# Down projection: the second block group takes six tiles in place of four, the plain group ahead of it two in place of four

## The chip, the cores and the metric

The kernel runs on one core of a Trainium2 chip. The metric is the device time of one execution in microseconds (us), the median of the runs; lower is better.

## The reference

Two layers of an encoder on 1040 frames (1024 and 16 learned ones in front) of width 1024. In each layer a mixing part (gated linear attention and softmax attention with a forget gate) is added to the residual `h`, and then a gated feed-forward part with a causal convolution. The change concerns the last product of that part, the down projection by `w_down`, from 2816 gated channels back to 1024:

```python
def conv_ffn(x, w_up, conv_w, conv_b, w_down):
    h = x @ w_up
    ...
    u, g = jnp.split(hc, 2, axis=-1)
    return (jax.nn.silu(g) * u) @ w_down
...
h = h + conv_ffn(rms_norm(h, ffn_norm[i]), w_up[i], conv_w[i], conv_b[i], w_down[i])
```

## The kernel before, in words

Everything is float32. A factor is split into a high part in TensorE's reduced format and a low part (the rest), and each product is three matmuls (`mm3`): high by high (L261), low weight by high (L262), high weight by low (L263). ScalarE makes the high part with a cast, VectorE the low part with a subtraction. Activations lie with channels on the 128 partitions and frames along the free axis.

**Tiles of the down projection.** The gated activation has 22 tiles of 128 channels; each was written to DRAM (`actd`) when it was made. The output has 8 tiles (m = 0 to 7), `hm0` to `hm7`, which hold the residual in DRAM. The two halves of the frames have 520 columns each in layer 0, which take two matmuls of 260, and 512 in layer 1, which take one. The 22 tiles are gone through in groups, listed in `GROUPS` as (kind, first tile, number of tiles); the last three tiles (`LAST`, 19 to 21) belong to `down_last`, which is not changed.

- A plain group (`"n"` or `"r"`, function `plain`) makes for each output tile and each half one product: all its gated tiles, three matmuls and one or two pieces each, into one of four two-bank PSUM tiles, p((2m+h) mod 4). The kind `"n"` copies the result out and adds it to `hm` in DRAM by an accumulating DMA of GpSimd (L1717). The kind `"r"` adds it on VectorE (L1713) into the residual tile `h0` to `h7`, which `load_residual` (L1688) has asked for on SP's queue.
- A block group (`"s"`, function `down_blocks`) takes its tiles as two halves (nk = half their number), two output tiles (2j and 2j+1) and two halves of the frames as a 2 by 2 block product, and makes seven products (p = 1 to 7) where eight would stand, from sums and differences of weights and of activations. Products of four pairs j run one after the other in a sequence that overlaps neighbouring pairs. The operands of the activations are `x1` to `x7`: `prepare` loads the gated tiles (`st`), combines them (L1546) and splits them (ScalarE L377, VectorE L378), in rounds of up to two tiles of each half. The weights come by `block_raws` (L1129) and `block_operand` (combinations at L1144, split at L1162 and L1163), asked for four products ahead (`AHEAD`); only for nk = 2 the raw weights of the next pair are asked for earlier (`ensure`). The results are `du` (tile 2j) and `dg` (tile 2j+1). `hand_on` adds them to `hm` by an accumulating DMA of GpSimd (L1617, before the residual is loaded) or to the residual tile on VectorE (L1614, after).

The order is: plain group of tiles 0 to 2, block group 3 to 10, plain group, block group, last three tiles.

**What sets the order.** TensorE's instructions stand in the order in which the program writes them. The other engines' instructions are ordered by a scheduler from the same text, so they shift with the code. All large tiles (`st`, `ah`, `al`, `x1` to `x7`, `du`, `dg`, `h0` to `h7`) share one list of 33 slots: `Slots.get` takes the slot that came free first, and a new user of a slot waits until its last user is done with it. For a `du` or `dg` of the first block group, that is when its accumulating DMA has landed.

```python
id = next((i for i in self.free if i in first), None) or next(i for i in self.free if i not in self.lent)
...
hT.append(s.get(F32, f"h{k}", first=ids))
nc.sync.dma_start(hT[k][:, o0:T], self.hm[k][:, o0:T])
...
nc.gpsimd.dma_start(self.hm[m][:, o0:T], x[:, o0:T], accum_op=ALU.add)
going.append((i + LANDING, x))
```

`pump` lets `prepare` run on whenever enough slots are free, so operands of the second block group are made during the first block group and the plain group behind it.

Of the kernel before, what the change touches and what calls it, by code (L numbers as in the profile page):

```python
# [48 lines left out]

GROUPS, LAST = (("n", 0, 3), ("s", 3, 8), ("r", 11, 4), ("s", 15, 4)), (19, 3)
HALVES, HALVES_LAST, HALVES_OUT = (0, 520, 520), (8, 524, 516), (16, 528, 512)
AHEAD = 4
LANDING = 4
# [1894 lines left out]
```

## Time and profile before

| | before |
|---|---|
| median of 3 runs | 2471.43 us (2471.32 to 2474.28) |
| the profiled execution | 2473.53 us, its span in the trace 2471.5 us |
| mean granted TensorE clock | 0.998 |
| plain group of four tiles, layer 0 | 1119.6 to 1165.5 us |
| second block group, layer 0 | 1165.5 to 1205.8 us |
| plain group of four tiles, layer 1 | 2340.5 to 2384.7 us |
| second block group, layer 1 | 2384.7 to 2423.6 us |

Times in rows are us from the span's start, unless marked ns. PE is TensorE, PEld its weight loads, DVE is VectorE, ACT is ScalarE, POOL is GpSimd, SP is SyncE, whose queue carries the loads. In a row of a timeline stand start, duration, engine, line, operation, output<-inputs without their numbers, shape and count, and in brackets the idle time of the engine before it and what released it. In a row of windows stand the window, the sum and each engine's busy time (with its count of instructions), the granted clock (1.00 is full speed), the DMA engines' busy share and GB/s. "st<-actd SPq ... , 260.0 KB, 3.7" is a group of transfers with the size of one and the median time from issue to landing.

### The profile page before, as it was taken

To read this page: it belongs to the slowest core of one execution; us is meant where nothing else is said; L and a number is where in the kernel's file an instruction comes from. 1 tells how busy PE (TensorE), PEld (TensorE's weight loads), DVE (VectorE), ACT (ScalarE), POOL (GpSimd) and SP (SyncE) were. 2 spreads that over 40 slices of the span, in tenths; PEclk is the share of its full clock that TensorE was granted. 3 is DMA by queue.
4 is the path that set the end of the run, shared out by engine and by line. 5 is a ranking of instruction groups with operands and counts; after the bars stand their busy time and mean duration, and the time that the engine had idled before them with its cause. 6 is when DMAs were issued, how large, how long until landed. Compare 5 with 4: busy or idle time off the path is not lost.

```text
span 2471.5 us, 47309 instructions
## 1 busy us (share of the span) xinstructions
PE 2440.1 (99%) x18286; PEld 2358.4 (95%) x18286; DVE 1873.4 (76%) x3769; ACT 1318.1 (53%) x2857; POOL 384.9 (16%) x565
## 2 busy tenths in 40 slices
PE   9999999999999999999999999999999999999998
PEld 8999999999999999999999999999999999998887
DVE  8665776869988888855866666777699888887667
ACT  7345766646555555642543456666465555556433
POOL 2023433210000000100220234331100000001002
PEclk9999999999999999999999999999999999999999
DMA  3222134443322224764312222243433212247722
GB/s 131 74 84 76 43 95 130 126 124 104 119 76 83 83 73 144 185 161 140 118 47 74 80 78 71 71 142 108 146 84 116 91 65 90 82 151 184 210 71 88
DMA packets 121680, 260.39 MB, mean 105 GB/s; under 512 B 15248, under 2 KB 37008, under 8 KB 121456
## 3 DMA queue, kind: packets, MB, share of 16 engines
q1 hardware_dynamic: 97008, 182.18, 23.8%
q0 software_dynamic: 22288, 72.81, 10.5%
q8 instruction: 143, 2.34, 0.4%
q10 hardware_dynamic: 2160, 2.38, 0.3%
q14 instruction: 81, 0.66, 0.1%
HBM read 176.74 MB, written 67.80 MB: 99 GB/s over the span
## 4 chain that ended last, share of the span: by engine, by line
PE 48%; issue 31%; DVE 13%; ACT 4%; DMA 2%; POOL 1%; SPq 0%; DVEq 0%; POOLq 0%; ACTq 0%
PE mm L261 7%; PE mm L263 7%; PE mm L262 7%; PE down L262 4%; PE down L261 4%; PE down L263 4%; PE av L780 3%; PE tr L754 2%; PE S L718 1%; DVE x L1188 1%; DVE S L721 1%; PE S L719 1%; ACT P L733 1%; DVE lo L1163 1%; DMA raw<-in_wm_dram 1%
## 5 line engine op out<-in xcount | busy, mean ns | idle before, releaser
L262 PE MATMUL up<-x,lo 128*128 128x260 f32 x2240 | 632.0, 282 | 0.9 <-DVE lo L1163 0.8
L261 PE MATMUL up<-x,hi 128*128 128x260 f32 x2240 | 632.0, 282 | 0.1
L263 PE MATMUL up<-x,hi 128*128 128x260 f32 x2240 | 632.0, 282 | 0.0
L262 PEld LDWEIGHTS up<-x,lo 128*128 128x128 f32 x2240 | 421.9, 188 | 1.4 <-DVE lo L1163 1.3
L261 PEld LDWEIGHTS up<-x,hi 128*128 128x128 f32 x2240 | 421.9, 188 | 0.4 <-ACT hi L1162 0.3
L263 PEld LDWEIGHTS up<-x,hi 128*128 128x128 f32 x2240 | 422.1, 188 | 0.0
L1162 ACT CAST hi<-raw 128x512 fp32r<-128x512 f32 (+1 forms) x490 | 266.3, 553 | 208.5 <-PE up L263 89.6
L261 PE MATMUL mm<-xh,hi 128*128 128x348 f32 (+6 forms) x1056 | 359.8, 341 | 0.0
L1163 DVE TENSOR_TENSOR lo<-raw,hi 128x512 fp32r<-128x512 f32 (+1 forms) x490 | 286.8, 600 | 81.3 <-ACT hi L1162 80.8
L263 PE MATMUL mm<-xl,hi 128*128 128x348 f32 (+6 forms) x1056 | 339.7, 322 | 0.0
L262 PE MATMUL mm<-xh,lo 128*128 128x348 f32 (+6 forms) x1056 | 338.7, 321 | 0.0
L261 PEld LDWEIGHTS mm<-xh,hi 128*128 128x128 f32 x1056 | 199.5, 189 | 2.3 <-issue 1.4
L262 PEld LDWEIGHTS mm<-xh,lo 128*128 128x128 f32 x1056 | 199.4, 189 | 0.3
L263 PEld LDWEIGHTS mm<-xl,hi 128*128 128x128 f32 x1056 | 198.6, 188 | 0.1
L1144 DVE TENSOR_TENSOR raw<-raw,raw 128x512 f32<-128x512 f32 (+1 forms) x230 | 146.8, 648 | 28.9 <-DMA raw<-in_wd_dram 26.3
L733 ACT ACTIVATE P<-S,m 116x460 f32<-116x460 f32 (+2 forms) x224 | 124.9, 562 | 77.1 <-DVE m L721 74.3
L228 ACT CAST hi<-raw 128x512 fp32r<-128x512 f32 (+2 forms) x152 | 87.4, 576 | 140.5 <-PE mm L263 59.6
L262 PE MATMUL down<-x,lo 128*128 128x260 f32 (+1 forms) x504 | 161.2, 320 | 0.6 <-DVE lo L1163 0.6
L263 PE MATMUL down<-x,hi 128*128 128x260 f32 (+1 forms) x504 | 161.2, 320 | 0.0
L261 PE MATMUL down<-x,hi 128*128 128x260 f32 (+1 forms) x504 | 161.1, 320 | 0.0
L378 DVE TENSOR_TENSOR PT<-tr,PT 116x464 fp32r<-116x464 f32 (+3 forms) x240 | 123.1, 515 | 48.9 <-ACT PT L377 47.2
L1424 POOL DMA_DIRECT2D actd<-cv x44 | 23.6, 535 | 734.5 <-DVE cv L1423 734.5
(313 smaller groups left out, 5957.8 us busy)
## 6 DMA issues: line engine op xcount, KB each, us to landing
raw<-in_wm_dram SPq DMA_DIRECT2D x326, 256.0 KB, 3.0
raw<-in_wd_dram SPq DMA_DIRECT2D x48, 256.0 KB, 4.4
actd<-cv POOLq DMA_DIRECT2D x22, 520.0 KB, 3.0
actd<-cv POOLq DMA_DIRECT2D x22, 512.0 KB, 2.9
cb<-cd SPq DMA_DIRECT2D x16, 520.0 KB, 3.9
kA<-kA SPq DMA_DIRECT2D x24, 260.0 KB, 4.0
kL<-kL SPq DMA_DIRECT2D x24, 260.0 KB, 4.7
st<-actd SPq DMA_DIRECT2D x24, 260.0 KB, 3.7
```

Source lines behind the costliest of these rows:

```text
L228: nc.scalar.copy(hi[:, :n, :], raw[:, :n, :])
L261: nc.tensor.matmul(ps, wh, xh[:, c0:c0 + n], start=first, stop=False, skip_group_check=more)
L262: nc.tensor.matmul(ps, wl, xh[:, c0:c0 + n], start=False, stop=False, skip_group_check=more)
L263: nc.tensor.matmul(ps, wh, xl[:, c0:c0 + n], start=False, stop=last, skip_group_check=more)
L378: nc.vector.tensor_tensor(out=lo, in0=src, in1=hi.bitcast(F32), op=ALU.subtract)
L718: nc.tensor.matmul(S[:rows, :n], q["qA"][e][:, qs], q["kA"][e][:, c0:k1], start=True, stop=False)
L733: nc.scalar.activation(P[:rows, :n], S[:rows, :n], AF.Exp, scale=-1.0, bias=m[:rows, nch - 1:nch], accum_out=(den if nch == 1 else d3[:row ...
L754: nc.tensor.transpose(tr[:w, 3 - j, :rows], P[:rows, o:o + w], id_)
L780: nc.tensor.matmul(av[:, a:b], w.rearrange("p a b -> p (a b)"), x, start=(t == ts[0] and part == 0 and i == 0), stop=(t == last and i == 1))
L1144: nc.vector.tensor_tensor(out=q[out][:, :nk, :], in0=q[a][:, :nk, :], in1=q[b][:, :nk, :], op=op)
L1162: nc.scalar.copy(hi[:, :nk, :], src[:, :nk, :])
L1163: nc.vector.tensor_tensor(out=lo[:, :nk, :], in0=src[:, :nk, :], in1=hi[:, :nk, :].bitcast(F32), op=ALU.subtract)
```

## The change

One line. The second plain group takes tiles 11 and 12 alone, and the second block group tiles 13 to 18 (nk = 3, so rounds of two and of one tile in its operands, and weights of 3 × 128 columns). The last three tiles stay as they are.

```diff
-GROUPS, LAST = (("n", 0, 3), ("s", 3, 8), ("r", 11, 4), ("s", 15, 4)), (19, 3)
+GROUPS, LAST = (("n", 0, 3), ("s", 3, 8), ("r", 11, 2), ("s", 13, 6)), (19, 3)
```

The low parts of all these weights and activations are VectorE's in both versions. Two places show how it moves other engines' work. The first is VectorE at the start of the plain group in layer 0, before the change: the last `du` of the first block group (`du_14266`, L1622), the operands x4 and x3 of the second one (128x1040), and the first evacuations into the residual tiles (L1713), two for each output tile; `lo` is the low part of plain weights (L230).

```order
L1622 TENSOR_TENSOR du_14266<-down_14490,du_14266 128x520
L378 TENSOR_TENSOR x4_14664<-st_14341,x4_14663 128x1040
L1713 TENSOR_TENSOR h0_14590<-down_14606,h0_14590 128x520
L378 TENSOR_TENSOR x3_14726<-st_14344,x3_14725 128x1040
L1713 TENSOR_TENSOR h0_14590<-down_14632,h0_14590 128x520
L230 TENSOR_TENSOR lo_14670<-raw_14667,hi_14669 128x512
L1713 TENSOR_TENSOR h1_14592<-down_14673,h1_14592 128x520
L1713 TENSOR_TENSOR h1_14592<-down_14699,h1_14592 128x520
L230 TENSOR_TENSOR lo_14734<-raw_14731,hi_14733 128x512
L1713 TENSOR_TENSOR h2_14594<-down_14737,h2_14594 128x520
```

The same place after it, up to a little ahead of the first evacuation into `h2`:

```order
L1622 TENSOR_TENSOR du_14260<-down_14488,du_14260 128x520
L378 TENSOR_TENSOR x1_14677<-st_14339,x1_14677 128x520
L1713 TENSOR_TENSOR h0_14588<-down_14604,h0_14588 128x520
L378 TENSOR_TENSOR x3_14640<-st_14271,x3_14639 128x1040
L1713 TENSOR_TENSOR h0_14588<-down_14618,h0_14588 128x520
L230 TENSOR_TENSOR lo_14646<-raw_14643,hi_14645 128x256
L1713 TENSOR_TENSOR h1_14590<-down_14649,h1_14590 128x520
L378 TENSOR_TENSOR x2_14680<-st_14343,x2_14680 128x520
L1713 TENSOR_TENSOR h1_14590<-down_14663,h1_14590 128x520
L230 TENSOR_TENSOR lo_14686<-raw_14683,hi_14685 128x256
L378 TENSOR_TENSOR x6_14720<-t2_14718,x6_14720 128x520
L1546 TENSOR_TENSOR st_14339<-st_14345,t2_14718 128x520
```

`x7_14761` (128x520) and then `h2_14592` come next. x3 stands at the same place (now in the slot of `dg` whose accumulating DMA goes to `hm7`), and the second round of operands (x1, x2, x6, ..., 128x520) stands between the evacuations of a group that is half as long.

The second place is SP's queue at the same time, the loads of the residual tiles, before:

```order
L1688 DMA h2_14594<-hm2_106 128x1040
L1688 DMA h1_14592<-hm1_105 128x1040
L1688 DMA h3_14596<-hm3_107 128x1040
L1688 DMA h4_14598<-hm4_108 128x1040
L1688 DMA h5_14600<-hm5_109 128x1040
L1688 DMA h0_14590<-hm0_104 128x1040
L1487 DMA st_14729<-actd20_132 128x1040
L219 DMA raw_14789<-in_wd_dram 128x512
L1688 DMA h7_14604<-hm7_111 128x1040
L219 DMA raw_14847<-in_wd_dram 128x512
L1487 DMA st_15316<-actd21_133 128x1040
L1688 DMA h6_14602<-hm6_110 128x1040
```

and after:

```order
L1688 DMA h0_14588<-hm0_104 128x1040
L1688 DMA h3_14594<-hm3_107 128x1040
L1688 DMA h1_14590<-hm1_105 128x1040
L1688 DMA h4_14596<-hm4_108 128x1040
L1688 DMA h5_14598<-hm5_109 128x1040
L1487 DMA st_14632<-actd19_131 128x1040
L219 DMA raw_14727<-in_wd_dram 128x256
L219 DMA raw_14768<-in_wd_dram 128x256
L1688 DMA h7_14602<-hm7_111 128x1040
L219 DMA raw_14807<-in_wd_dram 128x256
L1688 DMA h2_14592<-hm2_106 128x1040
L1688 DMA h6_14600<-hm6_110 128x1040
```

The load of `h2` has moved from the first place among the residual loads to the seventh: its slot is now that of the last `du` (`du_14260`), whose accumulating DMA goes to `hm6`. Layer 1 shows the same.

## The prediction

> **What bounds the kernel now.** First the page's busy times, then the tables of windows for the down projection, cut at the group boundaries.
>
> ```profile
> PE 2440.1 (99%) x18286; PEld 2358.4 (95%) x18286; DVE 1873.4 (76%) x3769; ACT 1318.1 (53%) x2857; POOL 384.9 (16%) x565
> ...
> 1119.60:1165.50 45.90, 45.90 (x386) 45.90 (x385) 11.06 (x16) 0.00 (x0) 1.00 0.40 120
> 1165.50:1205.80 40.30, 40.30 (x338) 40.22 (x336) 8.29 (x12) 9.52 (x16) 1.00 0.20 57
> 2340.50:2384.70 44.20, 44.20 (x194) 36.05 (x193) 10.91 (x16) 0.00 (x0) 1.00 0.42 121
> 2384.70:2423.60 38.90, 38.90 (x169) 31.36 (x167) 8.21 (x12) 9.38 (x16) 1.00 0.20 55
> ```
>
> TensorE is busy 99% of the span. The window rows (tile `down` alone; columns: window, then sum, PE, weight loads, DVE, ACT, granted clock, DMA share, GB/s) are the second plain group and the second block group, layer 0 and then layer 1. PE fills each window wholly at clock 1.00, so a matmul taken away shortens the kernel by its own time, as long as nothing makes PE wait. 384 matmuls of 260 columns in 45.9 us are 0.1196 us each; 192 of 512 columns in 44.2 us are 0.230 us each.
>
> **The change, part by part: fewer matmuls.** A tile costs 96 matmuls as plain and 84 in a block group in layer 0 (48 and 42 in layer 1, where a matmul covers 512 columns). Two tiles move, so 24 × 0.1196 = 2.87 us and 12 × 0.230 = 2.76 us go: −5.6 us.
>
> **The plain group is half as long, and what it waits for is not.** It starts here:
>
> ```profile
> 1119.62 0.28 PE L261 MATMUL down<-ah,hi 128*128 128x260 f32 x1
> ...
> 2340.53 0.39 PE L261 MATMUL down<-ah,hi 128*128 128x512 f32 x1
> ```
>
> The 16 products of the group (8 output tiles × 2 halves) go round four PSUM tiles, so product 8 (m=4, first half) waits for the evacuation of product 4 (m=2, first half), which adds it into `h2`. A product is now 12 matmuls (1.44 us; 6 of 0.230 are 1.38 us in layer 1), so product 8 is due at 1119.62 + 8 × 1.44 = 1131.1, and in layer 1 at 2340.53 + 8 × 1.38 = 2351.6. Before it was due only 8 × 2.87 = 23 us after the start. In the new order two things that stand ahead of that evacuation wait for accumulating DMAs of the first block group: the low part of x3 waits until `hm7<-dg` has landed (its slot), and the load of `h2`, moved from first place among SP's residual loads to seventh, waits until `hm6<-du` has landed (`h2` gets the slot of that `du`). The timelines of GpSimd, SP and VectorE (start, duration, idle before and its releaser) show when these land now:
>
> ```profile
> 1117.84 0.86 POOL L1617 DMA_DIRECT2D hm<-dg  x1 [9.27 <-ACT dg L1623]
> 1120.82 0.85 POOL L1617 DMA_DIRECT2D hm<-du  x1 [2.12 <-DVE du L1622]
> ...
> 1116.74 0.32 SPq L1688 DMA_DIRECT2D h<-hm  x1
> 1118.26 0.32 SPq L1487 DMA_DIRECT2D st<-actd  x1
> 1118.63 0.42 SPq L219 DMA_DIRECT2D raw<-in_wd_dram  x1
> 1127.24 0.32 SPq L1688 DMA_DIRECT2D h<-hm  x1
> ...
> 1130.52 0.32 SPq L1688 DMA_DIRECT2D h<-hm  x1
> ...
> 1130.62 1.24 DVE L378 TENSOR_TENSOR x<-st,x 128x1040 fp32r<-128x1040 f32 x1 [6.56 <-DMA hm<-du]
> 1131.78 0.69 DVE L1713 TENSOR_TENSOR h<-down,h 128x520 f32<-128x520 f32 x1
> ...
> 2341.89 0.86 POOL L1617 DMA_DIRECT2D hm<-du  x1 [1.95 <-DVE du L1622]
> ...
> 2347.86 0.32 SPq L1688 DMA_DIRECT2D h<-hm  x1
> 2350.45 0.32 SPq L1688 DMA_DIRECT2D h<-hm  x1
> ```
>
> SP's rows at 1127.24 and 1130.52 are `h7` and `h6`, released by those two landings (2347.86 and 2350.45 in layer 1). VectorE already stood idle 6.56 us for one of them; that cost nothing, because PE's products were twice as long. Why they land late is seen in the windows of all instructions and in the DMA issues (last number: us to landing), the quiet pair being the group's own earlier accumulates:
>
> ```profile
> 1105.40:1121.60 16.20, 16.20 (x137) 16.20 (x137) 15.99 (x18) 9.03 (x11) 2.48 (x3) 1.00 1.00 307
> 1113.60:1121.20 7.60, 7.60 (x66) 7.60 (x65) 7.39 (x9) 4.30 (x5) 1.24 (x2) 1.00 1.02 414
> 1121.20:1130.50 9.30, 9.30 (x81) 9.30 (x80) 1.17 (x2) 1.58 (x2) 0.47 (x1) 1.00 1.02 264
> ...
> q0 software_dynamic: 5, 0.02, 2.9%
> ...
> hm<-dg POOLq DMA_DIRECT2D x1, 520.0 KB, 9.4
> hm<-du POOLq DMA_DIRECT2D x1, 520.0 KB, 9.7
> ...
> hm<-dg POOLq DMA_DIRECT2D x1, 520.0 KB, 5.6
> hm<-du POOLq DMA_DIRECT2D x1, 520.0 KB, 6.2
> ...
> hm<-du POOLq DMA_DIRECT2D x1, 512.0 KB, 8.5
> ...
> h<-hm SPq DMA_DIRECT2D x1, 520.0 KB, 4.3
> ...
> h<-hm SPq DMA_DIRECT2D x1, 512.0 KB, 4.4
> h<-hm SPq DMA_DIRECT2D x1, 512.0 KB, 5.5
> ```
>
> Until 1121.2 the six residual loads fill the DMA engines at 414 GB/s and the software queue gets 0.02 MB of its transfers (row of 1117.5 to 1122); then both kinds share 264 GB/s. In the new order five residual loads instead of six run ahead there: one tile of 0.53 MB at 414 GB/s, 1.3 us earlier. So I take `hm6<-du` at 1130.52 − 1.3 = 1129.2; the load of `h2` at 4.0 us (between 4.3 here and the 3.7 of the page's row below, since less runs beside it); the evacuation 0.69: 1133.9, a stall of 2.8 us. Layer 1: 2350.45 − 1.2 + 4.0 + 0.69 = 2353.9, a stall of 2.3 us. Sum +5.1 us.
>
> ```profile
> st<-actd SPq DMA_DIRECT2D x24, 260.0 KB, 3.7
> ...
> L1163 DVE TENSOR_TENSOR lo<-raw,hi 128x256 fp32r<-128x256 f32 x28 | 11.0, 417 | 2.4 <-ACT hi L1162 2.3
> ```
>
> The ends: with the quiet 6.2 us and the quiet load of 3.7, 1120.82 + 6.2 + 3.7 + 0.7 = 1131.4 and 2341.89 + 6.2 + 3.7 + 0.7 = 2352.5, 0.3 + 0.9 = 1.2 us in all. With landings as now and loads of 4.3 and 5.5, 1135.5 and 2356.6: 4.4 + 5.0 = 9.4 us. The value lies nearer the middle because the loads ahead of the accumulates are still mostly there. The Trainium skill ("DMA: Bandwidth & Descriptors", section "Queues, rings and completion order") has each DMA engine take packets from the queue rows in turn. By that rule the accumulates would have half of the engines soon after their issue, land near the quiet times, and the sum of stalls would be near 1.2 us; the row with 0.02 MB for the software queue speaks against it here, so it only carries the lower end.
>
> **VectorE's new work around it.** The second block group now has three tiles in each half, so its operands come in a round of two and a round of one: seven more low parts and four more combinations of 128x520, about 0.6 us each (half of the 1.24 us above), 6.8 us, against two plain low parts of 1.24 fewer. Nearly all of it stands behind the last `du`, where VectorE had 6.56 us of idleness; with 16 evacuations of 0.69 = 11.0, these 6.8, x3's 1.24 and weight parts (six of 0.42 as in the row of 256 columns above, eight of 384 columns at about 0.55), 6.9 us, it has 26 us to do in a plain group of 23.0 us plus the stall. I cost it at nothing, because evacuations of m=3 to m=7 stay due one after another and PE's own stall gives VectorE the time; if the cover fails, it is the excess, 26 − 23.0 − 2.8, that is up to 0.5 us a layer, and it grows with every us that x3 starts later.
>
> **Block weights.** They are 384 wide, where they were 256:
>
> ```profile
> 1165.50:1205.80 40.30, 40.30 (x339) 40.30 (x338) 32.15 (x58) 22.34 (x48) 0.00 (x0) 1.00 0.20 57
> ```
>
> VectorE's 32.15 us in the second block group would be at most 48.2 if all of it grew by a half; the group itself grows from 40.3 to 60.4 us. The early fetch of the next weights (only for groups of four) is lost: they are now asked for four products ahead, 4 × 18 × 0.1196 = 8.6 us, against a landing of 4.4 us (page: raw, below) and three or four VectorE steps no longer than a 128x520 one (0.69). Hidden, with 0 to 1 us at each of two boundaries a layer as the other end. The first weights of the last three tiles now take slots that the last block product frees; two output tiles of 9 matmuls stand between, at 400 columns 18 × 0.1196 × 400/260 = 3.3 us, against two casts and two low parts of about 0.55, 2.2 us: nothing, or up to 1 us.
>
> ```profile
> raw<-in_wd_dram SPq DMA_DIRECT2D x48, 256.0 KB, 4.4
> 1060.00:1095.00 35.00, 35.00 (x294) 35.00 (x293) 16.07 (x24) 11.61 (x20) 3.40 (x4) 1.00 0.68 160
> ```
>
> The loads of tiles 13 and 14 and of the operands move into the first block group, where DMA moves 160 GB/s against 414 later, and POOL issues four transfers in 35 us: nothing, and were this cover gone, one tile's 1.3 us.
>
> **Sum.** The profiled execution took 2473.53 us, 2.1 above the median of 2471.43. −5.6 + 5.1 = −0.5: 2473.0 against it, and 2470.9 against the median.
>
> **Rivals.** 0.2% of the time, 4.9 us, is about what a measurement of this kernel can tell from no change.
> (a) The accumulates come in the quiet time: the stalls are 0 to 1.2 us, −5.6 to −4.4: 2465.8 to 2467.0. For it: the two earlier accumulates took 5.6 and 6.2 us. Against it: they ran before the residual loads, and these must run beside them.
> (b) The stall doubles. In the new order the load of tile 19 and two weight loads of 128 KB follow the residual loads, and could be on the queue before the accumulates' data, 0.79 MB / 0.414 = 1.9 us, less 1.3 for the missing tile: `hm6` lands 0.6 us later than before, stalls of 5.0 and 5.6, x3's low part as late, and VectorE's 26 us overrun by 0.5 each. 10.6 + 1.0 − 5.6 = +6.0: 2477.4, slower. It decides from stalls of 10.5 us on, that is landings more than about 0.6 us later than before. For it: the software queue got nothing while the others ran. Against it: the rows of st and raw at 1118.26 and 1118.63 did not stop the accumulates from 1121.2 on. The Trainium skill ("TensorE: Matmul & The Clock Gate", section "What's actually happening") adds that an idle window of about 3.4 us halves the clock until about as long a busy one has passed; by that page such stalls would cost some 1.7 us more each, an estimate from its figures. No row of the down projection here has PE idle or a clock under 1.00, so no run shows it.
> (c) Nothing waits, and the early landing as well as VectorE's work are wholly covered, with the end of the kernel held by another engine: 2471.4. PE's 99% speaks against it; it would be hard to tell from the forecast by time alone.
>
> **How the numbers follow.** Forecast, with stalls of 1.2 to 9.4 us (2467.0 to 2475.2) and (c) in it: 0.68, of which (c) 0.02. Rival (a): 0.14, of which nearly all under 2466.5. Rival (b): 0.18. So faster 0.14, same 0.68, slower 0.18. The range reaches from the middle of (a), 2466.0, to the near part of (b), 2476.5.
>
> **What would show it.** Right: 36 fewer matmuls; a PE gap of 2 to 3 us near product 8 of the plain group in each layer, ended by the evacuation L1713, VectorE idle before it with `h<-hm` as its releaser, the `hm<-du` ahead landing at about 1129 and 2349; PE unbroken in the second block group. Wrong: no gap (then −5.6); a gap ended by weight parts (L1163, L1144) in the block group; gaps of 5 us; or a clock under 1.00 behind the gap.

## The result: slower by 0.26%, and the profile after

The changed kernel took 2478.80 us (median of 7 runs, 2476.75 to 2483.00), the kernel before 2473.34 us (7 runs beside them): the ratio is 1.0026, 95% interval 1.0017 to 1.0035. Forecast was no change, 2470.9 us (2466.0 to 2476.5). A second measurement beside the experiments gave 2476.71 us and 1.0016 (1.0007 to 1.0025): slower both times, by 0.16 to 0.26%. One of the eleven runs of experiment 3 below took 3947.27 us at a granted clock of 0.556 and is left out of its ratio. The profiled execution has a span of 2476.7 us against 2471.5.

The page's busy times, and the windows of tile `down`: plain group and second block group, layer 0 and then layer 1, with the columns of the prediction's rows.

```profile
PE 2438.6 (98%) x18250; PEld 2356.2 (95%) x18250; DVE 1890.5 (76%) x3787; ACT 1325.9 (54%) x2867; POOL 385.1 (16%) x565
...
1118.50:1145.60 27.10, 25.11 (x195) 24.72 (x194) 10.03 (x15) 0.00 (x0) 0.94 0.76 221
1145.60:1205.90 60.30, 60.30 (x505) 60.21 (x504) 9.22 (x14) 9.52 (x16) 1.00 0.17 47
2342.00:2369.50 27.50, 24.20 (x98) 18.97 (x97) 10.73 (x16) 0.00 (x0) 0.94 0.72 203
2369.50:2427.90 58.40, 58.40 (x253) 47.10 (x251) 8.25 (x12) 9.40 (x16) 1.00 0.17 48
```

TensorE has 36 matmuls fewer (18,250 for 18,286). The block groups are filled wholly, at 0.1196 us a matmul in layer 0 (60.3 / 504). Plain groups of 23.0 and 22.1 us of work lasted 27.1 and 27.5, TensorE was idle 2.0 and 3.3 us in them, and the mean granted clock was 0.94 in both. From the start of the plain group to the end of the block group: 87.4 us against 86.2 before, and 85.9 against 83.1, together +4.0 us.

TensorE's rows at the gaps (layer 0, product 5; layer 1, products 5 and 8), VectorE's and SP's beside them, and two windows behind the gaps (tile `down`; the clock is the third column from the end):

```profile
1125.59 0.28 PE L263 MATMUL down<-al,hi 128*128 128x260 f32 x1
1127.75 0.39 PE L261 MATMUL down<-ah,hi 128*128 128x260 f32 x1 [1.88 <-DVE h L1713]
...
2350.26 0.50 PE L261 MATMUL down<-ah,hi 128*128 128x512 f32 x1 [1.22 <-DVE h L1713]
2356.77 0.47 PE L261 MATMUL down<-ah,hi 128*128 128x512 f32 x1 [2.08 <-DVE h L1713]
...
1125.84 1.24 DVE L378 TENSOR_TENSOR x<-st,x 128x1040 fp32r<-128x1040 f32 x1 [4.73 <-DMA hm<-dg]
1127.00 0.69 DVE L1713 TENSOR_TENSOR h<-down,h 128x520 f32<-128x520 f32 x1
...
1133.13 1.31 DVE L1713 TENSOR_TENSOR h<-down,h 128x520 f32<-128x520 f32 x2 [1.12 <-DMA h<-hm]
...
2355.93 1.29 DVE L1713 TENSOR_TENSOR h<-down,h 128x512 f32<-128x512 f32 x2 [1.45 <-DMA h<-hm]
...
1128.73 0.80 SPq L1688 DMA_DIRECT2D h<-hm  x2
...
2350.99 0.86 SPq L1688 DMA_DIRECT2D h<-hm  x2
...
1129.20:1132.60 3.40, 3.40 (x18) 3.40 (x17) 0.65 (x1) 0.00 (x0) 0.50 0.86 270
2358.00:2361.40 3.40, 3.40 (x9) 2.64 (x8) 1.88 (x3) 0.00 (x0) 0.50 0.55 170
```

Read from the bottom of the chain: x3's low part (1125.84) waited 4.73 us for `hm<-dg`; the second evacuation of `h0` (1127.00) stands behind it on VectorE; TensorE's product 5 needs the PSUM tile that it empties. Then SP issued `h2` at 1128.73, when `hm<-du` had landed, and VectorE waited for that load until 1133.13, the evacuation on which product 8 hangs. In the window from 1129.2 TensorE ran 18 matmuls in 3.4 us, 0.19 us each instead of 0.12, at clock 0.50. Layer 1 has its half clock behind product 8.

Product 8 started at 1133.98, 4.0 us later than 8 products behind the group's start at 1118.50, and in layer 1 at 2356.77, 3.8 us later (start 2341.97). In layer 0 the half clock lay before product 8 and cost nothing more, since `h2` set that start: only 0.28 us of gap was left there. In layer 1 it came behind it and added 1.6 us (8 matmuls at 0.427 instead of 0.230). So −5.6 + 4.0 + 3.8 + 1.6 = +3.8 of the +4.0 us.

### The profile page after: what moved, and what is told of

The parts are those of the page before. It is cut to its first block, busy times and chain, and to the rows that moved or that the text cites. A ratio compares the mean times of both kernels' runs of the same rounds, so it can differ in the third digit from the quotient of the medians.

```text
span 2476.7 us, 47296 instructions
## 1 busy us (share of the span) xinstructions
PE 2438.6 (98%) x18250; PEld 2356.2 (95%) x18250; DVE 1890.5 (76%) x3787; ACT 1325.9 (54%) x2867; POOL 385.1 (16%) x565
## 4 chain that ended last, share of the span: by engine, by line
PE 47%; issue 32%; DVE 13%; ACT 5%; DMA 3%; POOL 1%; SPq 0%; DVEq 0%; POOLq 0%; ACTq 0%
PE mm L261 7%; PE mm L263 7%; PE mm L262 7%; PE down L261 4%; PE down L262 4%; PE down L263 4%; PE av L780 3%; PE tr L754 2%; PE S L718 1%; DVE S L721 1%; PE wo L263 1%; PE wo L262 1%; PE wo L261 1%; PE S L719 1%; DVE lo L1163 1%
## 5 line engine op out<-in xcount | busy, mean ns | idle before, releaser
L1162 ACT CAST hi<-raw 128x512 fp32r<-128x512 f32 (+2 forms) x490 | 272.4, 565 | 193.7 <-PE up L263 89.6
L1163 DVE TENSOR_TENSOR lo<-raw,hi 128x512 fp32r<-128x512 f32 (+2 forms) x490 | 296.0, 617 | 82.5 <-ACT hi L1162 81.9
L261 PE MATMUL down<-x,hi 128*128 128x260 f32 (+1 forms) x588 | 187.9, 320 | 0.6 <-DVE dg L1622 0.6
L262 PE MATMUL down<-x,lo 128*128 128x260 f32 (+1 forms) x588 | 188.0, 320 | 0.2 <-DVE lo L1163 0.2
L263 PE MATMUL down<-x,hi 128*128 128x260 f32 (+1 forms) x588 | 187.9, 320 | 0.0
L1144 DVE TENSOR_TENSOR raw<-raw,raw 128x512 f32<-128x512 f32 (+1 forms) x230 | 152.0, 669 | 26.0 <-DMA raw<-in_wd_dram 23.4
L228 ACT CAST hi<-raw 128x512 fp32r<-128x512 f32 (+3 forms) x152 | 83.9, 553 | 114.9 <-PE mm L263 57.0
```

The lines of the kernel that those rows point to most:

```text
L228: nc.scalar.copy(hi[:, :n, :], raw[:, :n, :])
L261: nc.tensor.matmul(ps, wh, xh[:, c0:c0 + n], start=first, stop=False, skip_group_check=more)
L262: nc.tensor.matmul(ps, wl, xh[:, c0:c0 + n], start=False, stop=False, skip_group_check=more)
L263: nc.tensor.matmul(ps, wh, xl[:, c0:c0 + n], start=False, stop=last, skip_group_check=more)
L1144: nc.vector.tensor_tensor(out=q[out][:, :nk, :], in0=q[a][:, :nk, :], in1=q[b][:, :nk, :], op=op)
L1162: nc.scalar.copy(hi[:, :nk, :], src[:, :nk, :])
```

## The experiments

Each kernel is timed against runs of the kernel before beside it, on one chip; the first four share these runs (median 2472.25 us of 27), the last four share others, on another chip (2472.63 us of 33). One profiled execution stands for each kernel.

**1. h2 takes another slot.** `handed` keeps the slots of the last `du` (6) and `dg` (7).

```diff
+                self.handed[m] = x.id          # in hand_on, behind the accumulating DMA
 ...
+            late = [k for k in (6,) if self.handed.get(k) in s.free]
+            t = {k: s.get(F32, f"h{k}", first=[self.handed[k]]) for k in late}
             for k in range(KD):
-                hT.append(s.get(F32, f"h{k}", first=ids))
+                hT.append(t[k] if k in t else s.get(F32, f"h{k}", first=ids))
                 nc.sync.dma_start(hT[k][:, o0:T], self.hm[k][:, o0:T])
```

> The changed kernel, with h6 taking the slot of the last du, so that h2's load waits for no accumulate; x3's low part still waits for hm7. Theory A (two waits on accumulates, and a clock halved by the gap): the gap at product 5 of the plain group stays (about 2.0 us in layer 0 and 1.4 in layer 1), with half clock behind it for 3.4 us where the gap is long enough (+1.6 us); the gap at product 8 goes. Plain groups about 26.7 and 23.5 to 25.2 us, in place of 27.05 and 27.5; the whole 2.5 to 4.5 us below the changed kernel, about 2475. Theory B (VectorE's added work is the bound of the plain group, the slots don't matter): both groups stay above 27 us, time as the changed kernel, about 2479.

Measured: 2474.60 us, ratio 1.0012 (1.0003 to 1.0021). Windows of the two plain groups:

```profile
1117.20:1143.00 25.80, 23.36 (x194) 23.15 (x194) 10.20 (x15) 0.00 (x0) 1.00 0.76 225
2338.60:2363.30 24.70, 22.51 (x97) 17.75 (x96) 9.99 (x15) 0.00 (x0) 1.00 0.77 227
```

One gap a layer is left, 2.60 and 2.36 us at product 5, and the clock stayed at 1.00. Theory A had shorter gaps (2.0 and 1.4 us) and half clock at least in layer 0; the time of 2474.60 is what it gave. The gap at product 8 is gone, as in theory A. The groups lie below 27 us, so theory B falls.

**2. x3 takes another slot.** The same with `(7,)` in place of `(6,)`: `h7` gets the slot that x3's low part would have had.

> The changed kernel, with h7 taking the slot of the last dg, so that x3's low part waits for no accumulate; h2's load still waits for hm6. Theory A: no gap at product 5; one gap of 3.5 to 4 us at product 8 in each layer, ended by h2's landing, and half clock for 3.4 us behind it (+1.6 us). Plain groups about 28.4 and 27.4 us, time as the changed kernel or 1.5 us above: 2479 to 2480. Theory B: VectorE starts its work 5 us earlier, so gaps shrink below 1 us in all and the time falls to about 2471.

Measured: 2478.22 us, ratio 1.0027 (1.0017 to 1.0037). The plain groups, and TensorE's slow stretches:

```profile
1121.00:1148.40 27.40, 24.80 (x194) 24.62 (x193) 10.99 (x16) 0.00 (x0) 0.94 0.74 215
2345.00:2373.80 28.80, 24.62 (x97) 19.63 (x96) 10.79 (x16) 0.00 (x0) 0.88 0.67 189
...
1136.70:1139.90 3.20, 3.20 (x17) 3.20 (x16) 1.81 (x3) 0.00 (x0) 0.50 0.31 90
2360.70:2365.20 4.50, 4.50 (x11) 3.44 (x11) 2.09 (x4) 0.00 (x0) 0.50 0.56 169
```

No gap at product 5; one at product 8 of 2.76 us in layer 0 (less than forecast) and 4.34 in layer 1, each with half clock behind it (4.34 is more than forecast). VectorE's head start of five us didn't help, as theory A said: the two waits lie side by side. The wait for `h2` alone costs about as much as both (1.0027 beside 1.0026 and 1.0016), the wait for x3 alone (experiment 1) less. The profiled execution took 2482.93 us, 4.7 above the median, so its groups show rather much.

**3. Both.** With `(6, 7)`.

> The changed kernel with both slots changed: neither h2 nor x3 waits for an accumulate. Theory A: no gap over 0.3 us in the plain group, clock 1.00 throughout, plain groups 23.0 and 22.1 us; 9 us below the changed kernel and 4.5 to 5.6 us below the kernel before: about 2468. Theory B: gaps ended by VectorE evacuations remain, 1 to 2 us a layer or more, about 2471 or above.

Measured: 2468.89 us, ratio 0.9989 (0.9980 to 0.9998): faster than before by 3.4 us. The changed kernel stood 5.5 us above it in the first measurement and 4.1 us in the second, so the slots are worth 7.5 to 8.8 us in it.

```profile
1116.50:1139.60 23.10, 23.10 (x194) 23.10 (x193) 9.73 (x15) 0.00 (x0) 1.00 0.83 250
2335.20:2357.30 22.10, 22.10 (x97) 18.00 (x96) 9.78 (x15) 0.00 (x0) 1.00 0.86 258
```

TensorE fills both groups at clock 1.00, in the 23.1 and 22.1 us that its matmuls take. VectorE does as much work (36 instructions in layer 0's plain group in both kernels), in a somewhat different order, since its scheduler follows the text, and keeps up: theory B falls altogether. The edit changes that order too, and no run takes the two apart; that the gaps were ended by the loads and accumulates is read from the rows above.

**4. Filler in the gaps.** Products 4 and 7 of the plain group are computed twice.

```diff
-                for k in range(ng):
-                    for c in range(pieces):
-                        self.mm3(ps[:, c, :n], w[k], acts[g0 + k], halves[h] + c * n, n, k == 0, k == ng - 1)
+                for _ in range(2 if kind == "r" and (m, h) in ((2, 0), (3, 1)) else 1):
+                    for k in range(ng):
+                        for c in range(pieces):
+                            self.mm3(ps[:, c, :n], w[k], acts[g0 + k], halves[h] + c * n, n, k == 0, k == ng - 1)
```

> The changed kernel, but products 4 and 7 of the second plain group are computed twice (the second time restarts the sum), 1.4 us of extra TensorE work each, where TensorE otherwise waits behind them. Theory A: the starts of products 5 and 8 stay where they are, since evacuations set them; the idle stretches shrink to below 1 us and the granted clock stays 1.00; layer 0 unchanged in length (about 27.0 us, h2's landing sets it), layer 1 shorter by the 1.6 us of half clock (about 26.0); time about 2477. Rival C (the clock falls for another cause than the idle stretch, such as load or time): half clock remains for 3.4 us a layer, and the 24 extra matmuls of layer 0 and 12 of layer 1 cost nothing or up to 5.6 us: 2479 to 2484.

Measured: 2478.71 us, ratio 1.0030 (1.0019 to 1.0040).

```profile
1118.50:1147.60 29.10, 27.06 (x218) 26.22 (x217) 9.63 (x14) 0.00 (x0) 1.00 0.71 203
2343.90:2370.10 26.20, 25.17 (x110) 20.11 (x109) 9.58 (x14) 0.00 (x0) 1.00 0.73 213
```

No gap was over 1.2 us and the clock stayed at 1.00 in both layers, which fits the clock following idle TensorE and speaks against rival C, though one execution without half clock is weak evidence. The time is not the 2477 of theory A, and nearer to rival C's range. Layer 1 came down from 27.5 to 26.2 us. Layer 0 went up from 27.1 to 29.1: product 8 started 0.7 us later behind the group's start than in the changed kernel's profile, and a new gap of 0.9 us stood at product 11, ended by VectorE's evacuation of `h3`. Behind `h2` the evacuations are a queue of their own, and what the clock gives back is partly taken there. By time this kernel is no better than the changed one, so it doesn't price the half clock; by the rows of the changed kernel the half clock is 1.6 us of a loss of 5.2.

**5. The slots in the kernel before.** The same edit as in 3, groups as before.

> The kernel before with the two slot changes alone (h6 takes the slot of the last du, h7 that of the last dg). Theory A: nothing changes, since its plain group of four tiles has no gap: 2472.3, within 1.5 us. Rival: the slots are worth something by themselves (the 3.4 us by which the changed kernel with both slots beat the kernel before would then not be the moved tiles'): 2468 to 2469.

Measured: 2473.74 us, ratio 1.0004 (0.9996 to 1.0013); the plain groups are as long as they were (45.9 and 44.3 us), without a gap. The slots alone are worth nothing that the runs can tell; in experiment 3 they let the moved tiles pay.

**6. The raw weights first.** The kernel of experiment 3, with the transfers of the first block group's second pair and of the six tiles' operands kept in program order on SP. It was made because TensorE's waits in the changed kernel show one more place, in layer 0's first block group, where the profile before has none:

```profile
PE down L261 <- DVE dg L1622: 0.6, 1, 0.6
```

There the last raw weights of the pair stood behind three operand loads (`st`) on SP where one stood before. SP's timeline in the changed kernel, and in this experiment:

```profile
1041.86 1.68 SPq L1493 DMA_DIRECT2D st<-actd  x3
1043.63 0.44 SPq L1129 DMA_DIRECT2D raw<-in_wd_dram  x1
```

```profile
1042.10 0.33 SPq L1491 DMA_DIRECT2D st<-actd  x1
1042.52 1.69 SPq L1131 DMA_DIRECT2D raw<-in_wd_dram  x3
```

```diff
-                nc.sync.dma_start(q[name][:, :nk, :], src[:, k0:k0 + nk, :])
+                d = nc.sync.dma_start(q[name][:, :nk, :], src[:, k0:k0 + nk, :])
+                if nk == 4 and j == 1 and self.in_down:
+                    self.tc.keep_in_program_order(d)
 ...
-                nc.sync.dma_start(t[:, i, :W], self.actd[j0 + i][:, halves[h]:halves[h] + W])
+                d = nc.sync.dma_start(t[:, i, :W], self.actd[j0 + i][:, halves[h]:halves[h] + W])
+                if j0 >= 13:
+                    self.tc.keep_in_program_order(d)
```

> The changed kernel with both slots, and SP issuing the raw weights of the first block group's second pair ahead of the operand loads of tiles 13 to 18, as in the kernel before. Theory D (besides the two waits, the moved operand loads delay those weights and cost a gap of 0 to 1.7 us in layer 0's first block group, in some executions): no gap over 0.1 us in the first block group, 0.6 us on average below the kernel with both slots, about 2468.3. Rival: those gaps have another cause and are still there in size and place, no change in time.

Measured: 2468.28 us, ratio 0.9986 (0.9977 to 0.9995), the lowest median of all. In layer 0's first block group no gap is left, but experiment 3 had none there either, with the changed kernel's order on SP, so this run alone shows little, and 0.6 us of time is below what the runs can tell. Layer 1 has a new gap of 0.5 us in its first block group. The ten traces together say more. The landing of the pair's last raw weights (issue on SP plus time to landing), counted from the start of the block group, beside the gap (us):

| | before | exp. 5 | exp. 6 | exp. 3 | exp. 7 | exp. 1 | exp. 4 | changed, second | changed, first | exp. 2 |
|---|---|---|---|---|---|---|---|---|---|---|
| operand loads (`st`) just ahead on SP | 1 | 1 | 0 | 3 | 3 | 3 | 3 | 3 | 3 | 3 |
| landing | 14.75 | 14.57 | 13.82 | 14.74 | 14.78 | 14.99 | 15.13 | 15.39 | 15.50 | 16.40 |
| gap | none | none | none | none | none | 0.25 | 0.39 | 0.66 | 0.77 | 1.67 |

Each gap is the landing less 14.73 to 14.74 us. So theory D has the wait right: the late weights make the gap. The order on SP moves the landing towards that edge, but doesn't put it past it in every execution; what it costs in the median time is not shown.

**7. Slots in layer 0 alone.** `((6, 7) if lyr == 0 else ())` in experiment 3.

> The changed kernel with both slots changed in layer 0 alone. Theory A, additive by layer: layer 0's plain group 23.0 us without a gap, layer 1's 27.5 us with gaps at products 5 and 8 and the half clock: about 5.4 us above the kernel with both slots in both layers, 2474.3. Rival: the clock or the gaps of layer 1 hang on those of layer 0: 2469 or 2479.

Measured: 2474.15 us, ratio 1.0005 (0.9996 to 1.0014).

```profile
1119.40:1142.50 23.10, 23.10 (x194) 23.10 (x193) 9.73 (x14) 0.00 (x0) 1.00 0.83 248
2337.90:2363.70 25.80, 22.71 (x98) 17.85 (x97) 9.96 (x15) 0.00 (x0) 1.00 0.76 218
```

The median lies where theory A put it, 5.3 us above experiment 3. Layer 0 is clean, layer 1 keeps its two gaps (2.0 and 1.4 us), in this execution without half clock, so its group is 25.8 us and not 27.5. As far as the runs can tell, the layers' losses add up.

**8. The changed kernel again.**

> The changed kernel once more, for a second profile beside the others on one chip: gaps at products 5 and 8 of the plain group in both layers, x3's and h2's landings as their causes, 3.4 us at clock 0.50 behind at least one gap; 2478.8 us, 5 to 6 us above the kernel before.

Measured: 2476.71 us, ratio 1.0016 (1.0007 to 1.0025). Plain groups and the slow stretch:

```profile
1118.10:1147.00 28.90, 25.17 (x195) 24.78 (x194) 10.95 (x16) 0.00 (x0) 0.94 0.72 209
2341.60:2367.00 25.40, 22.72 (x98) 17.86 (x97) 9.95 (x15) 0.00 (x0) 1.00 0.76 222
...
1134.10:1137.50 3.40, 3.40 (x18) 3.40 (x17) 1.69 (x4) 0.00 (x0) 0.50 0.48 142
```

Gaps at products 5 and 8 in both layers, as expected (2.0 and 2.1 us; 1.6 and 1.4); half clock in layer 0 alone, of these groups. The sum of the two groups, 54.2 us, is that of the first profile, 54.6, though spread otherwise. The distance of 4.1 us to the kernel before is less than the 5 to 6 expected.

## Why the prediction was wrong, by its steps

- **Fewer matmuls, −5.6 us: right.** 36 matmuls are gone, and experiment 3, with the gaps gone, has groups of 23.1 and 22.1 us.
- **What the plain group waits for: right in place, short in size.** Both waits of the prediction are there, and experiments 1 to 3 show that they and nothing else hold TensorE. They made product 8 late by 4.0 and 3.8 us, where 2.8 and 2.3 stood in the sum: this term was 2.7 us short, inside its bounds of 1.2 to 9.4. Two pieces of it failed. The accumulate ahead of `h2` landed 10.2 and 9.0 us behind the group's start (rows 1128.73 and 2350.99, starts 1118.50 and 2341.97), against 10.9 and 9.9 before: with one residual tile fewer on the queue it came 0.7 and 0.9 us earlier, not 1.3 and 1.2. And the load of `h2`, taken at 4.0, took 4.3 and 4.8 us; some 0.3 us a layer more went by from landing over the evacuation to TensorE's start:

```profile
h<-hm SPq DMA_DIRECT2D x1, 520.0 KB, 4.3
...
h<-hm SPq DMA_DIRECT2D x1, 512.0 KB, 4.8
```

- **The gap at product 5** was named as a wait, with x3 behind `hm7`, but had no term; it is the larger of the two gaps in layer 0. Alone it left the kernel at 1.0012 (experiment 1), alone the other left it at 1.0027 (experiment 2): side by side, not one behind the other, so leaving it out of the sum is not what failed.
- **The clock: wrong.** It had no term in the forecast, and stood only as an addition to a slower rival. It cost about 1.6 us in one layer of each profile of the changed kernel. A gap of 2.0 us was enough (row 1127.75), so the forecast's own stall of 2.8 us was long enough to carry that price, though not in every execution (last section). The Trainium skill ("TensorE: Matmul & The Clock Gate", section "What's actually happening") asks for an idle window of about 3.4 us; the trace disagrees.
- **Loads moved into the first block group, 0: wrong in the profiles by 0.8 and 0.7 us.** A gap of that size stands there in both profiles of the changed kernel and none in that of before, and it follows the landing of the raw weights behind these loads (experiment 6). The step looked at what DMA moved on average, 160 GB/s, and not at who stands behind whom on SP.
- **VectorE's work, the weights of 384 columns, the lost early fetch, at 0: right.** The second block groups have no gap, in any of the profiles. VectorE's queue behind `h2` shows only once the clock is kept up (experiment 4).
- **The sum.** Forecast −0.5; by the first profile −5.6 + 7.8 + 1.6 + 0.8 is +4.6, in a span that grew by 5.2. So the forecast failed on the size of the stall (2.7 us short) and on two terms put at nothing, the clock (1.6) and the moved loads (0.8); the wait itself was foreseen. Rival (b) had the sign, through a landing later than before, but it landed earlier; rival (a) fell with the landings of 8.4 and 8.5 us:

```profile
hm<-dg POOLq DMA_DIRECT2D x1, 520.0 KB, 8.4
...
hm<-du POOLq DMA_DIRECT2D x1, 520.0 KB, 8.5
```

- **Open:** experiments 3 and 6 should stand 5 us below the kernel before by their groups, and their medians stand 3.4 and 4.3 below. The intervals reach to 4.9 and 5.7 us, so nothing need be missing. What a single execution shows scatters: experiment 3's profile has a stretch of half clock outside the changed code (last section), that of the kernel before has none.

## What to carry to other kernels

When a stage gets shorter, list what it waits for that does not get shorter, and look in the allocation for whose buffer each early load or operand takes: giving the tiles needed last the slots that come free last turned a loss of 0.16 to 0.26% into a gain of 0.11%. A short idle stretch on TensorE is to be priced with the half clock that may follow, about 1.6 us here, and with the queue that has built up on the engine that ends it. A load moved to an earlier place is to be checked against the transfers behind it in its own queue, not only against the mean use of the DMA engines.

## What the runs showed of the hardware that was not expected

Behind a gap the half clock lasted one stretch of 3.4 us, or two, 6.8 us, behind the gap of 4.34 us in experiment 2. The two stretches of the first profile start 1228.8 us apart (1129.2 and 2358.0), 360 times 3.413: as if a window runs on its own and judges each 3.4 us. That agrees with the free-running window of the same section of the Trainium skill. The other traces bear it out: in experiment 2, stretches start at 1136.61, 1327.76, 1686.16 and 2358.59 us, which are 56, 105 and 197 times 3.4133 us apart.

A gap did not need to fill a window: of nine gaps of about 2 us or more in the changed kernel's two profiles and experiments 1, 2 and 7, five had half clock behind them (2.04, 2.06, 2.25, 2.76 and 4.34 us) and four had not (1.99, 2.05, 2.36 and 2.60). The switches of the clock give the edges of the windows in each trace, and where the gap falls against them sorts these nine: the five left TensorE idle for 1.88 to 2.39 us inside one window, while the four met an edge and left at most 1.58 to 1.82 us inside one.

A wait outside the changed code shows the same. Between 1671 and 1685 us TensorE waits 1.74 to 1.75 us for VectorE in every one of the ten traces. The rows show it in experiment 3, with window edges at 1671.08, 1674.49 and 1677.91, and in experiment 6, where no half clock follows, with edges at 1672.68, 1676.10 and 1679.51 (all instructions; the clock is the third column from the end):

```profile
1674.12 0.38 PE L264 MATMUL mm<-ml,hi 128*128 128x256 f32 x1 [1.75 <-DVE ml L379]
...
1674.50:1677.90 3.40, 3.40 (x20) 3.40 (x18) 3.40 (x12) 3.40 (x9) 1.09 (x2) 0.50 0.36 94
...
1676.84 0.38 PE L265 MATMUL mm<-ml,hi 128*128 128x256 f32 x1 [1.74 <-DVE ml L380]
...
1676.10:1679.50 3.40, 2.66 (x23) 2.66 (x24) 3.40 (x13) 3.40 (x10) 1.09 (x2) 1.00 0.07 16
1679.50:1682.90 3.40, 2.32 (x19) 2.08 (x19) 3.40 (x10) 3.40 (x10) 0.56 (x1) 1.00 0.71 222
```

In experiments 1, 2, 3 and 7 the whole wait lies inside one window, and a stretch of half clock begins at that window's end. In the other six traces an edge cuts the wait (in the changed kernel's first profile by about 0.02 us only), and none follows. A like wait of about 1.76 us near 450 us lies inside one window in the changed kernel's second profile alone, and only there half clock follows. So the same wait costs half clock in one execution and nothing in the next. No single idle time sorts all cases, though: one window idle for 1.82 us had no half clock behind it, and the stretch at 1327.76 us in experiment 2 followed a window idle for 1.37 us. What else counts stays open.
